# Third tile's input loaded in 32x32 squares and turned by VectorE, with its first norm's sums by ones-products

## The chip, the cores and the metric

One core of a Trainium2 chip runs the whole program. The metric is device microseconds (us) of one execution; the median of several executions stands for a kernel. TensorE (PE) does matrix products, VectorE (DVE) elementwise work, ScalarE (ACT) activations with a scale and a bias, GpSimd (POOL) almost nothing here, and SyncE (SP) issues nearly all transfers (DMA).

## The reference

The reference is one step of a two-layer encoder over two groups of frames, 1024 "prompt" rows and 32 "sample" rows, each 1024 channels wide, with shared weights. What matters for this change is its beginning:

```python
def rmsnorm(x, g):
    xf = x.astype(jnp.float32)
    y = xf * lax.rsqrt(jnp.mean(xf * xf, axis=-1, keepdims=True) + EPS)
    return (y * g.astype(jnp.float32)).astype(x.dtype)
...
    for i in range(DEPTH):
        mod = jax.nn.silu(c) @ w_ada[i] + b_ada[i]
        sh1, sc1, gt1, sh2, sc2, gt2 = jnp.split(mod[:, None, :], N_MOD, axis=-1)
        h = rmsnorm(x, g_norm[i, 0]) * (1 + sc1) + sh1
        ...
            mix, v = sgu_mixer(h, ...)      # z = gelu(h @ w_in); u, v = split(z); v is normed again
        ...
        x = x + gt1 * rmsnorm(mix, g_norm[i, 1])
        h = rmsnorm(x, g_norm[i, 2]) * (1 + sc2) + sh2
        f = jnp.square(jax.nn.relu(h @ ffn_w_up[i])) @ ffn_w_down[i]
        x = x + gt2 * rmsnorm(f, g_norm[i, 3])
```

All arrays are float32. The sum of squares of the first norm runs over the 1024 channels of each token.

## The kernel before

The 1056 tokens are cut into three tiles: tiles 0 and 1 hold 384 prompt tokens each (three blocks of 128), tile 2 holds 256 prompt tokens and the 32 sample tokens (288 in all). On chip a tile lies with channels on the partitions: `acc[t]` is `[128, 8, 16 + n]`, eight channel blocks of 128 by n tokens behind a halo of 16 columns. Each float32 operand of a product is split into a high and a low part (`hh`/`hl` for the activations, `wh`/`wl` for the weights), and a product takes three matmuls: hi*hi, hi*lo, lo*hi.

**Blocks and items.** The nine token blocks are numbered b = 0 to 8; block 8 is the 32 sample rows. `stream` is one list of transfers in the order of their issue on SP's queue: x blocks (`"x", b`), weights of the conditioning (`"ada"`, 512 KB each) and pieces of the mixer's input weights (`"v", p, q`: columns p*512 to p*512+511 of the v half, channel blocks 2q and 2q+1; 512 KB each). `issue()` issues items until the next one needs one of the three `raw` buffers and none is free; each "v" item takes one and gives it back when `do_w` has split it (ACT copies the high part, L440; DVE subtracts for the low part, L79). `stream_to` works the list down to a named item.

**How x comes in.** A block is loaded with tokens on the partitions (`x_rows`, one 4 KB row for each token; block 8 goes into `junk`, the tile that also takes the discarded squares). `do_x` lets ACT square each row and add it up along the row (`x_squares`, L585, sums in `ssx`); `x_turn` turns the block by TensorE against the identity (L600, eight 128x128 transposes for a block, into PSUM), and DVE and ACT copy the halves into `acc[t]` (L606, L608). `first_norm(t)` is a generator: `spread` makes the factor 1/rms for each token from the sums (three tokens' blocks in three columns; DVE and ACT on 128x3), lays it on diagonals (L739), and three products with ones (L743, `pb_h`) spread it over all partitions; `apply` then multiplies by the coefficients (DVE, `mt`), adds the shift (ACT, `hh`, L890) and takes the low part (DVE, `hl`).

**The order of the beginning** is written out by hand in a `tc.manual_schedule()` block: every instruction is issued in the order in which the code names it. While tiles 0 and 1 come in, `early_mm` does the products of piece p = 0 for blocks 0 to 4 (L988). Then come the remaining turns (`while x_turns: turn()`, blocks 6, 7 and 8), the first part of tile 2's norm, the products of piece 0 for block 5 (`v_mm`, L943 to L945, 24 matmuls), the spread of tile 2's factor, and the ends of the blocks (`v_end`: gelu L955, square with a sum L956, store to DRAM L957). Behind the block the framework's scheduler orders the instructions: `v_order` runs piece 1 over blocks 0 to 5, then pieces 0 and 1 over blocks 6 to 8, then pieces 2 and 3 over all blocks. PSUM has three buffers (`pd`) for these blocks, so a block's products wait until the block three before it has been read.

`Stat` is the kernel's other way to a norm, used in all later norms: ACT squares each channel block of `acc` (L761), DVE adds the eight squares (L79), ACT and DVE split the sum in two parts (L791, L79), and two products with ones over the partitions (L806) give each partition the sum over all 1024 channels. ACT then takes the reciprocal root and its square (L810, L811), and DVE does one Newton step.

At the very end of the program the kernel already has a load of the kind that the change introduces: `load_last` (L1400) reads nine transfers of 32 partitions by 32 by 32 values, with runs of 128 bytes, and `turn_x` turns them by `turn32`, VectorE's transpose of 32x32 squares.

Of the kernel before, what the change touches and what calls it, by code (L numbers as in the profile page):

```python
# [11 lines left out]
AF = mybir.ActivationFunctionType  # L12
# [3 lines left out]
P = 128  # L16
D = 1024
KB = D // P
SEQ = 1024
DEC = 32  # L20
# [3 lines left out]
HALO = 16  # L24
# [3 lines left out]
NT = len(TILES)  # L28
# [6 lines left out]
def tile_stream_encoder_step(  # L35
# [25 lines left out]
    nc = tc.nc  # L61
    act = nc.scalar.activation
# [23 lines left out]
    turn32 = on_dve(nc.vector.transpose, 0.1, 930.0)  # L86
# [10 lines left out]
    ncol = [p + s for _, p, s in TILES]  # L97
# [103 lines left out]
    def bring(func):  # L201

        act(out=junk1, in_=epsT, func=func)
# [27 lines left out]
    ssx = sums[:, 0:9]  # L231
# [9 lines left out]
    def add_w(key, ap, shape):  # L241
        stream.append(("w", key, ap, shape))
# [34 lines left out]
    def add_x(b):  # L277
        if b < 8:
            ap = x_prompt[0, b * P : (b + 1) * P, :]
        else:  # L280
            ap = x_sample[0]
        stream.append(("x", b, ap, None))

    def v_item(p, q):
        return (
            ("v", p, q),
            sgu_w_in[0][q * 256 : (q + 1) * 256, SGU + p * 512 : SGU + (p + 1) * 512].rearrange(
                "(k p) f -> p k f", p=P
            ),
            (2, 512),  # L290
        )

    def w_vpiece(p):
        for q in range(4):
            add_w(*v_item(p, q))
# [65 lines left out]
            for b in range(3, 6):  # L361
                add_x(b)
    first_ada = len(stream)
    for b in range(6, 9):
        add_x(b)
    w_vpiece(1)
    rest += [(add_ada, 0, j) for j in range(16, 40)] + [(add_wide, 0, j) for j in range(40, 48)]
    some_ada(8)
    for p in range(2, 4):
# [26 lines left out]
    def in_raw(k):  # L396
# [4 lines left out]

    x_rows = [
        room("h", t, f"x_rows{t}")
        .rearrange("p k n -> p (k n)")[:, : ncol[t] // P * D]
        .rearrange("p (b k n) -> p b k n", k=KB, n=P)
        for t in range(NT)
    ]
    junk = room("l", NT - 1, "xsq")

    def issue():  # L410
        while state["issued"] < len(stream):
            k = state["issued"]
            kind, key, ap, shape = stream[k]
            if in_raw(k):
                if state["raw"] == RAW_SLOTS:
                    return
                state["raw"] += 1
                r = t_raw(f"raw{k}")
            elif kind == "x":
                r = x_rows[key // 3][:, key % 3] if key < 8 else junk[:, :, P : 2 * P]  # L420
            else:
                r = work.tile([P, 1024], F32, tag="W", bufs=W_SLOTS, name=f"raw{k}")
            if kind == "x":
                nr = P if key < 8 else DEC
                i = nc.sync.dma_start(r[:nr], ap.rearrange("t (k n) -> t k n", n=P))
            else:
                i = nc.sync.dma_start(r.rearrange("p (a b) -> p a b", a=shape[0]), ap)
            raws[k] = r
            loads[key] = i.ins
            state["issued"] += 1  # L430
# [150 lines left out]
            n -= 1  # L581

    def x_squares(b, r):
        nr = P if b < 8 else DEC
        act(  # L585
            out=junk[:nr, :, :P],
            in_=r[:nr],
            func=AF.Square,
            accum_out=ssx[:nr, b : b + 1],
        )  # L590

    def x_turn(b, r):
        t = min(b // 3, 2)
        c0 = (b - 3 * t) * P
        nr = P if b < 8 else DEC
        for half in range(2):
            pt = (ps_up if b == 4 else ps_ms)(f"xT{b}_{half}")
            for i in range(4):
                k = half * 4 + i
                nc.tensor.transpose(  # L600
                    pt[:, i * nr : (i + 1) * nr], r[:nr, k, :], ident[:nr, :nr]
                )
            dst = acc[t][:, half * 4 : half * 4 + 4, HALO + c0 : HALO + c0 + nr]
            src = pt[:, : 4 * nr].rearrange("p (a b) -> p a b", a=4)
            if half == 0 or t == 0:
                nc.vector.tensor_copy(dst, src)  # L606
            else:
                act(out=dst, in_=src, func=AF.Copy)  # L608
# [2 lines left out]
    x_turns = deque()  # L611

    def do_x(b, r):
        x_squares(b, r)
        if b < 3:
            x_turn(b, r)
        else:
            x_turns.append(lambda: x_turn(b, r))
# [283 lines left out]
    def first_norm(t):  # L902
        n = ncol[t]
        nb = 3
        cp = t_c(f"r_h0_{t}")
        got = []
        yield from spread(t, ssx[:, 3 * t : 3 * t + nb], f"h0_{t}", got, cp)
        act(out=cp[:, :n], in_=got[0][:, :n], func=AF.Copy)
        yield "statistics"
        yield from apply(t, 0, 0, 0, cp, keep=True)  # L910

    def products(ps, n, terms):

        last = len(terms) - 1
        tick(3 * len(terms) * (0.004 + n / 2265.0))
        for i, (wh, wl, rh, rl) in enumerate(terms):
            mm(ps[:, :n], wh, rh, start=i == 0, stop=False)  # L917
            mm(ps[:, :n], wh, rl, start=False, stop=False)  # L918
            mm(ps[:, :n], wl, rh, start=False, stop=i == last)  # L919
# [27 lines left out]
    def v_end(ps, p, b):  # L947
        m = P if b < 8 else DEC
        vt = t_x(f"vt{p}_{b}", [P, 512])
        z = ps  # L950
        if b == 8:
            act(out=vt[:m, :], in_=ps[m : 2 * m, :], func=AF.Copy)
            tt(out=vt[:m, :], in0=vt[:m, :], in1=ps[:m, :], op=ALU.add)
            z = vt
        act(out=vt[:m, :], in_=z[:m, :], func=AF.Gelu_apprx_tanh)  # L955
        act(out=ps[:m, :], in_=vt[:m, :], func=AF.Square, accum_out=ssqv[:m, b, p : p + 1])  # L956
        nc.sync.dma_start(vd[b * P : b * P + m, p * 512 : (p + 1) * 512], vt[:m, :])  # L957

    def statistics(h):
        while next(h) != "statistics":  # L960
            pass

    def stream_to(kind, key):
        k = max(i for i, s in enumerate(stream) if s[0] == kind and s[1] == key)
        while state["next"] <= k:
            stream_step()
        run_deferred()
# [2 lines left out]


    early_ps = [ps_dn(f"pv0_{b}") for b in range(3)]
    h0, h1, h2 = (first_norm(t) for t in range(NT))

    def early_mm(bs, q):

# [19 lines left out]
    def early_end(bs):  # L996
        for b in bs:
            v_end(early_ps[b], 0, b)
# [9 lines left out]
    def turn():  # L1008
        x_turns.popleft()()
# [9 lines left out]
    with tc.manual_schedule():  # L1019
        load_vectors(nc.scalar, 2, slice(0, 2))  # L1020
        issue()
        load_vectors(nc.gpsimd, 0, slice(0, 1))
        load_vectors(nc.gpsimd, 1, slice(0, 1))
        load_vectors(nc.gpsimd, 2, slice(2, 4))
        bring(AF.Silu)
        stream_to("x", 0)
        turn_conditions()
        stream_to("x", 2)
        bring(AF.Sqrt)
        next(h0)  # L1030
        next(h0)
        stream_to("ada", (0, 4, 0))
        turn_vectors()
        stream_to("ada", (0, 4, 1))
        next(h0)
        statistics(h0)
        fold()
        next(h0)
        stream_to("ada", (0, 0, 1))
        fold()  # L1040
        stream_to("w", ("v", 0, 0))
        next(h0)
        late_hi.pop()()
        next(h0)
        lo()
        early_mm((0, 1, 2), 0)
        stream_to("x", 5)
        next(h1)
        turn()
        next(h1)  # L1050
        stream_to("ada", (0, 5, 1))
        turn()
        fold()
        next(h1)
        statistics(h1)
        turn()
        early_ps.extend(ps_up(f"pv0_{b}") for b in (3, 4))
        next(h1)
        row(h1)
        stream_to("ada", (0, 1, 1))  # L1060
        next(h0)
        early_mm((3,), 0)
        fold()
        early_mm((4,), 0)
        for q in range(1, 4):
            stream_to("w", ("v", 0, q))
            row(h0)
            lo()
            next(h1)
            row(h1)  # L1070
            if q == 3:
                stream_to("x", 8)
            early_mm((0, 1), q)
            if q < 3:
                conditions(q + 1)
                fold()
                next(h0)
            early_mm((2,), q)
            if q < 3:
                fold()  # L1080
            early_mm((3, 4), q)
        while x_turns:
            turn()
        next(h2)
        ps = ps_ms("pv0_5")
        v_mm(ps, 0, 5, range(KB))
        next(h2)
        next(h2)
        early_end((0,))
        stream_to("w", ("v", 1, 1))  # L1090
        early_end((1, 2))
        stream_to("w", ("v", 1, 2))
        early_end((3,))
        stream_to("w", ("v", 1, 3))
        early_end((4,))
        statistics(h2)
        v_end(ps, 0, 5)
        for _ in h2:
            pass

# [630 lines left out]
```

## Time and profile before

| | |
|---|---|
| median of 3 runs | 2165.44 us (2163.97 to 2165.93) |
| profiled execution, its own time | 2163.59 us |
| span of the profiled execution | 2161.8 us |
| granted TensorE clock | 0.999 |
| TensorE busy | 2143.9 us (99%) |
| VectorE busy | 1423.9 us (66%) |
| ScalarE busy | 981.9 us (45%) |
| DMA | 311.77 MB, mean 144 GB/s |

All times in the profile are us from the start of the span; the remaining 1.8 us of the execution lie outside it. A row of the timeline gives start, duration, engine, line, operation and tiles, and in brackets the idle time before it with what ended it. Consecutive matmuls overlap, so their rate is read from their starts and not from their durations.

### The profile page before, as it was taken

The page shows a single profiled execution, that of the slowest core. Times are in us where ns is not written, and L with a number is a line of the kernel's source. Part 1 is how long each engine was busy: PE and PEld are TensorE (multiplying, and loading weights), DVE is VectorE, ACT ScalarE, POOL GpSimd, SP SyncE. Part 2 cuts the span into 40 slices and gives each one's busy share as a digit, 9 for nine tenths or more (in the row PEclk, how much of TensorE's full clock was granted, in tenths as well). Part 3 has the DMA queues.
Part 4 walks back from the last instruction along what each step waited for, and adds up shares of the span by engine and source line. Part 5 has one row for each costly group of instructions (what it writes and reads, how often), then busy time and mean ns, then how long its engine had stood idle before and what let it go on. Part 6 is the DMA issues. An engine that isn't in the chain of part 4 may idle for free.

```text
span 2161.8 us, 33186 instructions
## 1 busy us (share of the span) xinstructions
PE 2143.9 (99%) x13214; PEld 2079.8 (96%) x13214; DVE 1423.9 (66%) x2520; ACT 981.9 (45%) x1667; POOL 7.9 (0%) x20
## 2 busy tenths in 40 slices
PE   8999999999999999999999999999999999999998
PEld 6878999999999999999999999999999999999998
DVE  6787738467778549576757779869685553523375
ACT  5634332233456652324345566656564542322454
POOL 0000000000000000000000000000000000000000
PEclk9999999999999999999999999999999999999999
DMA  8486524353447444344545466465454541302243
GB/s 299 153 269 209 168 82 136 96 153 107 133 126 220 127 147 146 98 117 137 175 127 164 143 192 200 148 193 164 141 161 133 166 149 58 108 20 69 78 137 120
DMA packets 363263, 311.77 MB, mean 144 GB/s; under 512 B 20099, under 2 KB 325803, under 8 KB 363109
## 3 DMA queue, kind: packets, MB, share of 16 engines
q1 hardware_dynamic: 362852, 309.43, 46.6%
q8 instruction: 103, 1.69, 0.3%
q14 instruction: 52, 0.42, 0.1%
q10 hardware_dynamic: 128, 0.14, 0.0%
q0 software_dynamic: 128, 0.09, 0.0%
HBM read 278.95 MB, written 30.66 MB: 143 GB/s over the span
## 4 chain that ended last, share of the span: by engine, by line
PE 96%; DVE 2%; DMA 1%; ACT 1%; issue 0%; POOL 0%; POOLq 0%; ACTq 0%; DVEq 0%
PE pf L917 11%; PE pg L917 11%; PE pf L919 11%; PE pf L918 11%; PE pg L919 11%; PE pg L918 11%; PE pu L917 3%; PE pu L919 3%; PE pu L918 3%; PE po L917 3%; PE po L918 3%; PE po L919 3%; PE pv L943 2%; PE pv L944 2%; PE pv L945 2%; PE psp L1263 1%
## 5 line engine op out<-in xcount | busy, mean ns | idle before, releaser
L917 PE MATMUL pg<-fh,wh_dn 128*128 128x384 f32 (+1 forms) x1536 | 496.1, 323 | 0.0
L917 PE MATMUL pf<-hh,wh_up 128*128 128x384 f32 (+1 forms) x1536 | 494.4, 322 | 0.0
L919 PE MATMUL pf<-hh,wl_up 128*128 128x384 f32 (+1 forms) x1536 | 493.0, 321 | 1.2 <-DVE wl_up L79 1.2
L918 PE MATMUL pf<-hl,wh_up 128*128 128x384 f32 (+1 forms) x1536 | 493.1, 321 | 0.0
L918 PE MATMUL pg<-fl,wh_dn 128*128 128x384 f32 (+1 forms) x1536 | 492.5, 321 | 0.0
L919 PE MATMUL pg<-fh,wl_dn 128*128 128x384 f32 (+1 forms) x1536 | 492.5, 321 | 0.0
L79 DVE TENSOR_TENSOR wl_up<-raw,wh_up 128x1024 fp32r<-128x1024 f32 x152 | 185.8, 1223 | 169.1 <-ACT wh_up L440 169.1
L919 PEld LDWEIGHTS pf<-hh,wl_up 128*128 128x128 f32 x1536 | 288.6, 188 | 1.9 <-DVE wl_up L79 1.9
L917 PEld LDWEIGHTS pg<-fh,wh_dn 128*128 128x128 f32 x1536 | 288.3, 188 | 1.5 <-ACT fh L1169 0.4
L440 ACT ACTIVATE wh_up<-raw 128x1024 fp32r<-128x1024 f32 x152 | 161.2, 1060 | 282.3 <-PE pf L918 217.7
L918 PEld LDWEIGHTS pg<-fl,wh_dn 128*128 128x128 f32 x1536 | 288.3, 188 | 0.9 <-DVE fl L79 0.2
L918 PEld LDWEIGHTS pf<-hl,wh_up 128*128 128x128 f32 x1536 | 288.3, 188 | 0.4
L917 PEld LDWEIGHTS pf<-hh,wh_up 128*128 128x128 f32 x1536 | 288.2, 188 | 0.4
L919 PEld LDWEIGHTS pg<-fh,wl_dn 128*128 128x128 f32 x1536 | 288.2, 188 | 0.0
L79 DVE TENSOR_TENSOR acc<-acc,pg 128x384 f32<-128x384 f32 (+1 forms) x336 | 173.7, 517 | 151.2 <-PE pg L919 150.5
L440 ACT ACTIVATE wh_dn<-raw 128x1024 fp32r<-128x1024 f32 x152 | 160.9, 1060 | 209.8 <-PE pg L918 171.4
L79 DVE TENSOR_TENSOR wl_dn<-raw,wh_dn 128x1024 fp32r<-128x1024 f32 x152 | 185.8, 1223 | 82.7 <-ACT wh_dn L440 82.6
L79 DVE SCALAR_TENSOR_TENSOR aa<-raw,csil,aa 128x512 f32<-128x512 f32 (+1 forms) x364 | 203.2, 619 | 7.6 <-DMA raw<-in_w_ada_dram 7.3
L1345 ACT ACTIVATE r<-pf 128x384 f32<-128x384 f32 (+1 forms) x192 | 86.5, 450 | 197.7 <-PE pf L919 197.7
L79 DVE TENSOR_TENSOR fl<-r,fh 128x384 fp32r<-128x384 f32 (+1 forms) x192 | 100.0, 521 | 85.7 <-ACT fh L1169 84.2
L917 PE MATMUL pu<-hh,wh_u 128*128 128x384 f32 (+1 forms) x384 | 125.9, 328 | 0.0
L917 PE MATMUL po<-ush,wh_o 128*128 128x384 f32 (+1 forms) x384 | 123.5, 322 | 0.0
(268 smaller groups left out, 2923.2 us busy)
## 6 DMA issues: line engine op xcount, KB each, us to landing
raw<-in_ffn_w_up_dram SPq DMA_DIRECT2D x152, 512.0 KB, 3.9
raw<-in_ffn_w_down_dram SPq DMA_DIRECT2D x152, 512.0 KB, 3.5
raw<-in_w_ada_dram SPq DMA_DIRECT2D x96, 512.0 KB, 4.4
raw<-in_sgu_w_in_dram SPq DMA_DIRECT2D x40, 512.0 KB, 4.2
xd<-acc SPq DMA_DIRECT2D x8, 1536.0 KB, 7.8
raw<-in_sgu_w_out_dram SPq DMA_DIRECT2D x24, 512.0 KB, 3.6
xo_r<-xd SPq DMA_DIRECT2D x32, 384.0 KB, 3.3
vd<-vt SPq DMA_DIRECT2D x32, 256.0 KB, 4.3
```

The lines of the kernel that those rows point to most:

```text
L79: return op(out, *args, **kw)
L440: act(out=wh, in_=r, func=AF.Copy)
L917: mm(ps[:, :n], wh, rh, start=i == 0, stop=False)
L918: mm(ps[:, :n], wh, rl, start=False, stop=False)
L919: mm(ps[:, :n], wl, rh, start=False, stop=i == last)
L943: mm(ps[:m, :], a_h, wh[:, o : o + 512], start=k == 0, stop=False)
L944: mm(ps[:m, :], a_h, wl[:, o : o + 512], start=False, stop=False)
L945: mm(ps[:m, :], a_l, wh[:, o : o + 512], start=False, stop=k == KB - 1)
L1263: mm(sp[:, c * P : (c + 1) * P], vl[:, c, k * P : (k + 1) * P], wr[:, c * P : (c + 1) * P], start=True, stop=True,)
L1345: act(out=r[:, :n], in_=ps[:, :n], func=AF.Relu)
```

## The change

Blocks 6, 7 and 8 are no longer loaded as rows. Each group of 32 tokens is loaded by four transfers, one for each a = 0 to 3, of 32 tokens (on partitions 32a to 32a+31) by 8 channel blocks by 32 channels, in runs of 128 bytes: 16 transfers for block 6, 16 for block 7, 4 for block 8. In the stream they stand between the four items of piece 1: block 6, v(1,0), block 7, v(1,1), block 8, v(1,2), v(1,3). Tile 2's data is turned by nine VectorE transposes of 128x8x32 (`turn32`) directly into `acc[2]`; TensorE's transposes, the row sums on ACT and the copies of blocks 6 to 8 are gone. The first norm of tile 2 goes by `Stat` in a new generator `last_first_norm`, with its reciprocal root taken on ACT. In the hand-written order, v(1,0) is split before the last `early_mm` calls, the gelu table is loaded by `bring` ahead of tile 2's squares, and block 5's `v_end` comes before the statistics of tile 2.

```diff
@@ stream
-    for b in range(6, 9):
-        add_x(b)
-    w_vpiece(1)
+    for q in range(4):
+        if q < 3:
+            add_x(6 + q)
+        add_w(*v_item(1, q))
@@ x_rows
-        .rearrange("p k n -> p (k n)")[:, : ncol[t] // P * D]
-        .rearrange("p (b k n) -> p b k n", k=KB, n=P)
+        .rearrange("p k n -> p (k n)")
+        .rearrange("p (b k n) -> p b k n", k=KB, n=P if t < NT - 1 else 32)
@@ issue
-                r = x_rows[key // 3][:, key % 3] if key < 8 else junk[:, :, P : 2 * P]
+                r = x_rows[min(key // 3, NT - 1)]
+                r = r[:, key % 3] if key < 6 else r
...
-            if kind == "x":
-                nr = P if key < 8 else DEC
-                i = nc.sync.dma_start(r[:nr], ap.rearrange("t (k n) -> t k n", n=P))
+            if kind == "x" and key < 6:
+                i = nc.sync.dma_start(r, ap.rearrange("t (k n) -> t k n", n=P))
+            elif kind == "x":
+                for j in range(ap.shape[0] // 32):
+                    for a in range(4):
+                        i = nc.sync.dma_start(
+                            r[32 * a : 32 * a + 32, 4 * (key - 6) + j],
+                            ap[32 * j : 32 * j + 32].rearrange("s (k a m) -> s a k m", a=4, m=32)[:, a],
+                        )
@@ x_squares, x_turn: the cases for the 32 rows of block 8 are dropped
...
     def do_x(b, r):
+        if b >= 6:
+            return
         x_squares(b, r)
@@ behind first_norm
+    def last_first_norm(t):
+        for j in range(ncol[t] // 32):
+            turn32(acc[t][:, :, HALO + 32 * j : HALO + 32 * j + 32], x_rows[t][:, j])
+        yield False
+        st = Stat(t, f"h0_{t}")
+        for k in range(KB):
+            st.square(k)
+        yield False
+        got = []
+        yield from st.finish(got)
+        yield "statistics"
+        yield from apply(t, 0, 0, 0, got[0], keep=True)
...
-    h0, h1, h2 = (first_norm(t) for t in range(NT))
+    h0, h1 = (first_norm(t) for t in range(2))
+    h2 = last_first_norm(2)
@@ the hand-written order
             if q == 3:
-                stream_to("x", 8)
+                stream_to("w", ("v", 1, 0))
             early_mm((0, 1), q)
...
-        while x_turns:
-            turn()
+        bring(AF.Gelu_apprx_tanh)
+        next(h2)
         next(h2)
         ps = ps_ms("pv0_5")
         v_mm(ps, 0, 5, range(KB))
-        next(h2)
-        next(h2)
         early_end((0,))
         stream_to("w", ("v", 1, 1))
         early_end((1, 2))
...
         early_end((4,))
+        v_end(ps, 0, 5)
         statistics(h2)
-        v_end(ps, 0, 5)
         for _ in h2:
             pass
```

More of the change, by code (lines that the diff above doesn't have):

```diff
@@ L583, in x_squares @@
     def x_squares(b, r):
[L584 to L590, printed above, removed]
+        act(out=junk[:, :, :P], in_=r, func=AF.Square, accum_out=ssx[:, b : b + 1])
     def x_turn(b, r):
-        t = min(b // 3, 2)
+        t = b // 3
         c0 = (b - 3 * t) * P
-        nr = P if b < 8 else DEC
         for half in range(2):
@@ L599, in x_turn @@
                 k = half * 4 + i
[L600 to L604, printed above, removed]
+                nc.tensor.transpose(pt[:, i * P : (i + 1) * P], r[:, k, :], ident)
+            dst = acc[t][:, half * 4 : half * 4 + 4, HALO + c0 : HALO + c0 + P]
+            src = pt.rearrange("p (a b) -> p a b", a=4)
             if half == 0 or t == 0:
```

## The prediction

> **What bounds the kernel now.** I read the page's busy times first, then its chain, and then the timelines of the four engines around the change, 30 to 80 us.
>
> ```profile
> PE 2143.9 (99%) x13214; PEld 2079.8 (96%) x13214; DVE 1423.9 (66%) x2520; ACT 981.9 (45%) x1667; POOL 7.9 (0%) x20
> PE 96%; DVE 2%; DMA 1%; ACT 1%; issue 0%; POOL 0%; POOLq 0%; ACTq 0%; DVEq 0%
> ```
>
> TensorE works for 2143.9 of 2161.8 us, and 96% of the chain that ended last is TensorE. So a change pays by the TensorE time that it takes away, and costs by the TensorE idle time that it makes. The order behind the hand-written part is the same but for a few neighbours swapped up to about 155 us, so I take an earlier TensorE to stay earlier until the end, us for us. The stretch is this one, in the timeline of TensorE (start, duration):
>
> ```profile
> 57.29 1.07 PE L988 MATMUL pv<-wl_v,hh 128*128 128x512 f32 x4
> 58.20 2.04 PE L600 MATMUL xT<-ident,x_rows 128*128 128x128 f32 x16
> 60.17 0.72 PE L600 MATMUL xT<-ident,xsq 32*128 32x32 f32 x8
> 60.99 0.50 PE L943 MATMUL pv<-wh_v,hh 128*128 128x512 f32 x1
> ...
> 66.38 0.40 PE L945 MATMUL pv<-wh_v,hl 128*128 128x512 f32 x1
> 66.61 0.94 PE L743 MATMUL pb_h<-r_h,ones 128*128 128x128 f32 x6
> 67.48 0.50 PE L943 MATMUL pv<-wh_v,hh 128*128 128x512 f32 x1
> 67.97 0.50 PE L944 MATMUL pv<-wl_v,hh 128*128 128x512 f32 x1
> ```
>
> From the end of `early_mm` (58.20) to the first matmul of piece 1 (67.48) TensorE spends 2.79 us on tile 2's transposes, 5.62 us on the 24 matmuls of block 5 (0.23 us each), and 0.87 us on the spread `pb_h`. After its first matmul, piece 1 stands still for 0.26 us more (67.48 to 67.97 instead of 0.23).
>
> **What goes.** The transposes and `pb_h`: 2.79 + 0.87 = 3.66 us of TensorE. What comes on TensorE is two products with ones over 288 columns, 0.30 us each:
>
> ```profile
> L806 PE MATMUL pn_rs<-sc_rs,ones 128*128 128x288 f32 x1 | 0.3, 300 | 0.0
> L761 ACT ACTIVATE sq_rs<-acc 128x288 f32<-128x288 f32 x8 | 3.4, 440 | 1.8 <-DVE acc L79 1.8
> L79 DVE TENSOR_TENSOR sq_rs<-sq_rs 128x288 f32<-128x288 f32 x7 | 3.2, 452 | 0.0
> L791 ACT ACTIVATE sc_rs<-sq_rs,eps 128x288 fp32r<-128x288 f32 x1 | 0.5, 538 | 0.5 <-DVE sq_rs L79 0.5
> L79 DVE SCALAR_TENSOR_TENSOR sm_rs<-sq_rs,eps,sc_rs 128x288 fp32r<-128x288 f32 x1 | 0.5, 515 | 0.0
> ```
>
> So the most that can be won is 3.66 - 0.60 + 0.26 + some 0.1 of overlap, about 3.4 us. That is under 0.2% of the time (4.3 us), which is about what a measurement of this kernel can tell from no change. What is left of it depends on three things: when the squares of x land, how long the new chain on VectorE and ScalarE is, and what ScalarE's new order holds up.
>
> **When x lands.** SP's queue in this stretch, then the landings of two of these transfers (KB, us from issue to landing), then two windows (busy time of each engine, clock, DMA share, GB/s):
>
> ```profile
> 30.74 2.17 SPq L427 DMA_DIRECT2D raw<-in_sgu_w_in_dram  x1
> 32.96 1.11 SPq L425 DMA_DIRECT2D x_rows<-in_x_prompt_dram  x2
> 34.11 0.71 SPq L425 DMA_DIRECT2D xsq<-in_x_sample_dram  x1
> 34.93 17.71 SPq L427 DMA_DIRECT2D raw<-in_sgu_w_in_dram  x3
> ...
> raw<-in_sgu_w_in_dram SPq DMA_DIRECT2D x1, 512.0 KB, 8.5
> x_rows<-in_x_prompt_dram SPq DMA_DIRECT2D x1, 512.0 KB, 7.8
> ...
> 30.00:40.00 10.00, 9.85 (x69) 6.68 (x69) 7.54 (x19) 4.33 (x9) 0.00 (x0) 1.00 1.07 398
> 40.00:50.00 10.00, 10.00 (x70) 7.41 (x69) 6.50 (x16) 4.67 (x9) 0.00 (x0) 1.00 0.41 123
> ```
>
> Until 40 us the transfers are full (the DMA share is 1.07, 398 GB/s), and SP issues about one a microsecond, each held until the transfer eight before it has landed. From 40 us the share is 0.41: there is room. In the changed kernel the first eight squares take the places of the old x rows, from 32.96 on, behind what is queued, and the ninth waits for the piece issued at 30.74, which lands at about 40 (30.74 + 8.5 from the start of its issue). From there SP issues 30 more transfers: 8 squares, v(1,0), 16 squares, v(1,1), 4 squares. Their pace is nowhere in this stretch. I bound it by two other places of the trace, four 64 KB loads issued back to back and two loads of 1024 runs of 128 bytes (the end of the kernel has nine of these; each is four of the new ones):
>
> ```profile
> 148.09 0.43 SPq L1193 DMA_DIRECT2D wt<-in_sgu_w_s_dram  x1
> ...
> 149.53 0.46 SPq L1196 DMA_DIRECT2D bs<-in_sgu_b_s_dram  x1
> 2066.34 1.32 SPq L1400 DMA_DIRECT2D xraw<-xtd  x2
> q1 hardware_dynamic: 1687, 0.21, 42.3%
> cache<-in_cache_pool_dram SPq DMA_DIRECT2D x2, 30.0 KB, 2.5
> ```
>
> Four issues from 148.09 to 149.53 make 0.48 us each, the two of 1024 runs 0.66 us each. I take 0.48, because a new one has a quarter of the runs. The fourth row is of the window 2066.3 to 2069.5, in which only those loads moved: 42.3% of 16 engines for 3.2 us over 1687 packets is 12.8 ns for 128 bytes, so one new transfer (256 packets) occupies the engines for 0.2 us, less than its issue. A 30 KB load lands in 2.5 us. The last square is then on chip at 40 + 30 x 0.48 + 2.5 = 56.9 us; at 0.66 it is 62.3.
>
> **The new chain.** It starts when VectorE and ScalarE are through with the last pieces of tile 1 and with v(1,0):
>
> ```profile
> 47.14 1.05 ACT L440 ACTIVATE wh_v<-raw 128x1024 fp32r<-128x1024 f32 x1
> 50.98 1.22 DVE L79 TENSOR_TENSOR wl_v<-raw,wh_v 128x1024 fp32r<-128x1024 f32 x1
> 52.76 1.15 ACT L890 ACTIVATE hh<-mt,mod 128x384 fp32r<-128x384 f32 x2 [2.37 <-DVE mt L79]
> 53.41 1.15 DVE L79 SCALAR_TENSOR_TENSOR hl<-mt,mod,hh 128x384 fp32r<-128x384 f32 x2 [0.16 <-ACT hh L890]
> 63.06 1.28 ACT L955 ACT_TABLE_LOAD   x1
> 64.36 0.60 ACT L955 ACTIVATE vt<-pv 128x512 f32<-128x512 f32 x1
> 65.62 1.99 ACT L440 ACTIVATE wh_v<-raw 128x1024 fp32r<-128x1024 f32 x2
> 89.66 0.76 DVE L79 STREAM_TRANSPOSE raw<-aa 128x256 f32<-128x256 f32 x2
> 90.35 0.60 DVE L79 SCALAR_TENSOR_TENSOR hl<-mt,mod,hh 128x256 fp32r<-128x256 f32 x2
> ```
>
> v(1,0) is issued after 16 squares, at about 44, so it is there at 53.9. ScalarE ends its `hh` at 53.9, the high part of v(1,0) at 54.9, and loads the gelu table (1.28) until 56.2; VectorE takes the low part (1.22) until 56.1. The nine turns are of 256 columns like the row at 89.66, two of which give way after 0.69 us: 9 x 0.35 = 3.2, until 59.3. The squares of x at 56.9 are in time for that; they are late from a pace of 0.55 us on. Then eight squares on ScalarE, 0.40 each back to back (between the row's 0.44 and 0.34 if it overlaps like the wider forms): 62.6. The last addition ends at 63.1, the split's first part (0.54) at 63.65, its second (0.52) at 64.2. TensorE, without the transposes, has block 5 done at 58.20 + 5.6 = 63.8, its first product with ones at 64.1, the second at 64.5.
>
> **What ScalarE holds up.** Piece 1 block 0 needs the PSUM buffer of piece 0 block 0, which ScalarE now reads only after the chain: gelu and square, 1.26 us (64.36 to 65.62 in the rows above), from 63.65 to 64.9. TensorE starts piece 1 at 64.9, 2.6 us earlier than before. Its eighth matmul there now is block 1's first, by the changed kernel's order of instructions. It waits for ScalarE's high part of v(1,1) (64.9 to 65.9) and the next gelu and square, until 67.2, while seven matmuls end at 66.5: 0.7 us idle. The low parts of v(1,2) and v(1,3) come out within 0.1 us of their use: 0.1 more. Before, that place lost 0.26. The gain is 2.6 - 0.8 + 0.26, so 2.0 us.
>
> **What is moved later.** Tile 2's factor now needs two more table loads on ScalarE (reciprocal root, then gelu again), behind the end of block 5.
>
> ```profile
> 75.28 0.60 ACT L955 ACTIVATE vt<-pv 128x512 f32<-128x512 f32 x1 [2.06 <-DMA vd<-vt]
> 76.97 0.65 DVE L79 SCALAR_TENSOR_TENSOR mt<-acc,coef,r_h 128x256 f32<-128x256 f32 x2 [1.35 <-ACT r_h L908]
> 91.38 0.72 ACT L890 ACTIVATE hh<-mt,mod 128x256 fp32r<-128x256 f32 x2 [1.05 <-DVE mt L79]
> ```
>
> Block 4's gelu waited until 75.28 for a store of SP's queue that stood behind v(1,3); v(1,3) is now ahead of all stores, so that I put this gelu at about 72. Two ends of blocks at 1.26, two loads at 1.28 and some 2.4 for root, gelu, square and VectorE's two steps put the factor at 79.5, where the first row with it was at 76.97. Tile 2's last `hh` (92.1 before) comes at about 95. TensorE needs tile 2 from 64.9 + 0.8 + 6 x 5.5 = 98.7 on, so 3 us of cover hide this. Of VectorE's additions (nine turns, seven sums, about 6 us, against 2.5 of copies and small steps dropped) all lie in a stretch where it was idle from 54.6 to 58.8 and from 62.1 to 66.7: no cost.
>
> **The sum.** The profiled execution took 2163.59 us, 1.85 under the median of 2165.44. Less 2.0 that is 2161.6 for an execution like it, and 2163.4 for a median.
>
> **Rivals.** *Late squares, slower.* If a new transfer costs SP not 0.48 us but what the full queue costs here, landing time over eight in flight, 7.8 / 8 = 0.98, then the last square lands at 40 + 30 x 0.98 + 2.5 = 71.9. The ninth turn starts 13 us later than 58.9, and ScalarE, VectorE and TensorE all stand in line behind it, since the gelu of block 0, the split of v(1,1) and the ones-products come after it on their queues. That is 2.0 - 13.0, a loss of 11 us: 2176.4. At 0.66 us it would be 1.4 us slower than before (2166.8); it decides from 0.55, and passes 0.2% at 0.76. For it: 36 transfers stand in place of three on one queue. Against it: the share of 0.41 from 40 us on, and 2.5 us for a small load, which with eight in flight is 0.31, below the issue. [...]
>
> *A longer chain, about no change.* If ScalarE's squares, the hand-overs between engines or the store that frees block 4's buffer take 2 us longer than the rows say, TensorE stands at the ones-products, and the gain is 0 plus or minus 1: 2165.4.
>
> *All of it.* If piece 1 finds ScalarE ready, 3.4 us: 2162.0. Against it speaks the gelu behind the split.
>
> **How the numbers follow.** Forecast (1 to 3 us won) 0.53, late squares 0.21, longer chain 0.15, all of it 0.11. Faster by over 0.2% would need all of it and the runs' scatter of 1 us: 0.07. Slower by over 0.2%: late squares from 0.76 us of pace on, 0.19. Within 0.2%: 0.74. The range reaches from all of it less 0.5 of scatter, 2161.5, past the pace of 0.66 (2166.8) and into the late squares up to 0.75, 2169.5; the forecast's own is 2162.3 to 2164.5.
>
> **What would show it.** Right: the last turn on VectorE at about 59.3, with no wait for a transfer of more than 1 us before it; the first matmul of piece 1 at 65, block 6 of piece 1 without a wait near 98.7. Wrong: a wait of the turns for `in_x_prompt_dram` beyond 60, issues of the squares over 0.55 us apart, or TensorE idle for more than 2 us between 63 and 75 or near 98.

## The result, and the profile after

| | before | changed |
|---|---|---|
| median of 22 runs each, us | 2163.32 (2162.48 to 2165.93) | 2166.88 (2165.86 to 2168.03) |
| ratio, 95% interval | | 1.0015 [1.0009, 1.0021] |
| profiled execution, us | 2163.59 | 2165.90 |
| its span, us | 2161.8 | 2164.1 |

The change makes the kernel 0.15% slower, 3.56 us by the medians. The forecast was 2.0 us faster. TensorE's busy time fell by 1.6 us, about half of the 3.1 that the change takes off (3.66 less 0.60), since the matmuls at half clock, shown below, last longer (3.56 us for nine, 0.40 each, against 7.60 for 35, 0.22 each); its share of the chain fell by a point, and SP's queue is new there (page of the changed kernel, busy times and chain):

```profile
PE 2142.3 (99%) x13186; PEld 2078.3 (96%) x13186; DVE 1429.2 (66%) x2531; ACT 982.6 (45%) x1667; POOL 7.9 (0%) x20
PE 95%; DVE 2%; DMA 2%; SPq 1%; ACT 1%; issue 0%; POOL 0%; POOLq 0%; DVEq 0%; ACTq 0%
```

The timeline of TensorE in the changed kernel (start, duration; in brackets the idle time before and what ended it), from the last of `early_mm` to the first matmul of piece 1, and on to the first of block 8:

```profile
57.79 1.07 PE L1004 MATMUL pv<-wl_v,hh 128*128 128x512 f32 x4
58.70 0.39 PE L958 MATMUL pv<-wh_v,hh 128*128 128x512 f32 x1
...
63.91 0.39 PE L960 MATMUL pv<-wh_v,hl 128*128 128x512 f32 x1
67.50 0.40 PE L808 MATMUL pn_h<-sc_h,ones 128*128 128x288 f32 x1 [3.20 <-ACT sc_h L793]
68.05 0.40 PE L808 MATMUL pn_h<-sm_h,ones 128*128 128x288 f32 x1 [0.16 <-DVE sm_h L79]
68.74 0.60 PE L958 MATMUL pv<-wh_v,hh 128*128 128x512 f32 x1 [0.28 <-ACT pv L971]
...
114.24 0.39 PE L950 MATMUL pv<-wh_v,hs 128*64 128x512 f32 x1
```

The transposes are gone: block 5 starts at 58.70, right behind `early_mm`. But the products with ones wait 3.20 us for ScalarE's part of the split. Piece 1 starts 10.04 us after `early_mm` (68.74 less 58.70); before it was 9.28 (67.48 less 58.20). That is 0.8 us of the loss; the larger part comes behind it:

```profile
64.20:67.50 3.30, 0.10 (x2) 1.00 0.17 66
68.70:72.30 3.60, 3.56 (x9) 0.54 0.27 82
72.40:80.00 7.60, 7.60 (x35) 1.00 0.83 243
```

These are windows of the changed kernel (length, TensorE's busy time and matmuls, granted clock, DMA share, GB/s). Behind its wait, which I call a stand, TensorE gets half its clock for 3.4 us (69.0 to 72.4), and does nine matmuls in 3.6 us, where 35 take 7.6 us later. Block 8 begins 55.5 us behind `early_mm`, against 53.5 before, by this row of the kernel before (111.66 less 58.20):

```profile
111.66 0.39 PE L935 MATMUL pv<-wh_v,hs 128*64 128x512 f32 x1
```

That distance is used below for every version, since the start-up ahead of it moves by up to 1.6 us from one profile to the next. Why the products wait stands in the timelines of SP, VectorE and ScalarE of the changed kernel, one after another:

```profile
32.98 12.34 SPq L431 DMA_DIRECT2D x_rows<-in_x_prompt_dram  x16
45.42 0.53 SPq L436 DMA_DIRECT2D raw<-in_sgu_w_in_dram  x1
46.00 10.33 SPq L431 DMA_DIRECT2D x_rows<-in_x_prompt_dram  x16
56.44 0.53 SPq L436 DMA_DIRECT2D raw<-in_sgu_w_in_dram  x1
57.02 3.08 SPq L431 DMA_DIRECT2D x_rows<-in_x_sample_dram  x4
```

```profile
56.53 2.40 DVE L79 STREAM_TRANSPOSE acc<-x_rows 128x256 f32<-128x256 f32 x7
59.56 0.45 DVE L79 STREAM_TRANSPOSE acc<-x_rows 128x256 f32<-128x256 f32 x1 [0.63 <-DMA x_rows<-in_x_prompt_dram]
61.76 0.45 DVE L79 STREAM_TRANSPOSE acc<-x_rows 128x256 f32<-128x256 f32 x1 [1.75 <-DMA x_rows<-in_x_sample_dram]
63.04 3.83 DVE L79 TENSOR_TENSOR sq_h<-sq_h 128x288 f32<-128x288 f32 x7 [0.84 <-ACT sq_h L763]
67.48 0.52 DVE L79 SCALAR_TENSOR_TENSOR sm_h<-sq_h,eps,sc_h 128x288 fp32r<-128x288 f32 x1 [0.60 <-ACT sc_h L793]
```

```profile
62.24 2.78 ACT L763 ACTIVATE sq_h<-acc 128x288 f32<-128x288 f32 x8 [5.36 <-DVE acc L79]
66.91 0.53 ACT L793 ACTIVATE sc_h<-sq_h,eps 128x288 fp32r<-128x288 f32 x1 [1.90 <-DVE sq_h L79]
67.35 0.58 ACT L970 ACTIVATE vt<-pv 128x512 f32<-128x512 f32 x1
```

SP issues the second sixteen squares in 10.33 us, 0.65 us each, without a wait between them, though each lands some 2.4 us after its issue, so that only about four are under way. It is through with the last square at 60.10. VectorE waits for it until 61.76. ScalarE waits 5.36 us ahead of its squares, with the ends of blocks 0 to 2 ready behind them in its queue. VectorE's seven additions take 3.83 us, one after another (each adds into the same tile), so ScalarE waits 1.90 us again before the split. Only then (67.35) comes the gelu that frees piece 1's first buffer.

### The profile page after: what moved, and what is told of

Its sections match the earlier page's. It is cut to its first block, busy times and chain, and to the rows that moved or that the text cites. A ratio compares the mean times of both kernels' runs of the same rounds, so it can differ in the third digit from the quotient of the medians.

```text
span 2164.1 us, 33199 instructions
## 1 busy us (share of the span) xinstructions
PE 2142.3 (99%) x13186; PEld 2078.3 (96%) x13186; DVE 1429.2 (66%) x2531; ACT 982.6 (45%) x1667; POOL 7.9 (0%) x20
## 4 chain that ended last, share of the span: by engine, by line
PE 95%; DVE 2%; DMA 2%; SPq 1%; ACT 1%; issue 0%; POOL 0%; POOLq 0%; DVEq 0%; ACTq 0%
PE pf L932 11%; PE pf L934 11%; PE pf L933 11%; PE pg L932 11%; PE pg L934 11%; PE pg L933 11%; PE po L932 3%; PE po L934 3%; PE po L933 3%; PE pu L932 3%; PE pu L934 3%; PE pu L933 3%; PE pv L958 2%; PE pv L960 2%; PE pv L959 2%; PE psp L1277 1%
```

## The experiments

Two theories stood against each other. *Late squares and a longer chain*: SP's 36 issues bring the last square too late, the sums take longer than I reckoned, and TensorE stands at the products with ones. *ScalarE*: what costs is the new order on ScalarE and its two more table loads. Each set of runs has its own runs of the kernel before. "Distance" is that from the end of `early_mm` to block 8's first matmul.

| version | median, us | kernel before | ratio, 95% interval | distance, us |
|---|---|---|---|---|
| before | | 2163.32 | | 53.5 |
| changed | 2166.88 | 2163.32 | 1.0015 [1.0009, 1.0021] | 55.5 |
| e1: 12 transfers | 2163.8 | 2163.14 | 1.0002 [0.9994, 1.0011] | 53.1 |
| e2: wait filled | 2166.81 | 2163.14 | 1.0017 [1.0008, 1.0025] | 56.1 |
| e3: no table loads | 2167.58 | 2163.14 | 1.0017 [1.0008, 1.0026] | 55.7 |
| e4: rows, new norm | 2164.85 | 2163.14 | 1.0006 [0.9997, 1.0015] | 54.0 |
| e5: other order | 2162.34 | 2163.48 | 0.9997 [0.9988, 1.0006] | 52.7 |
| e6: e5 with 12 transfers | 2161.63 | 2163.48 | 0.9989 [0.9980, 0.9998] | 49.9 |
| e8: e4 with that order | 2162.93 | 2163.48 | 0.9997 [0.9988, 1.0006] | 52.5 |
| e9: e6, start kept busy | 2160.39 | 2164.19 | 0.9983 [0.9974, 0.9992] | 49.8 |
| e10: before, start kept busy | 2163.48 | 2164.19 | 0.9998 [0.9989, 1.0007] | 53.5 |
| e11: changed, start kept busy | 2167.19 | 2164.19 | 1.0015 [1.0006, 1.0024] | 57.6 |

**e1, twelve transfers instead of 36.** Token 4s+j goes to square j, so that one transfer brings a partition group of four squares; the turns write with a step of four.

```diff
-                for j in range(ap.shape[0] // 32):
-                    for a in range(4):
-                        i = nc.sync.dma_start(
-                            r[32 * a : 32 * a + 32, 4 * (key - 6) + j],
-                            ap[32 * j : 32 * j + 32].rearrange("s (k a m) -> s a k m", a=4, m=32)[:, a],
+                nj = ap.shape[0] // 32
+                for a in range(4):
+                    i = nc.sync.dma_start(
+                        r[32 * a : 32 * a + 32, 4 * (key - 6) : 4 * (key - 6) + nj].rearrange("p j k m -> p (j k) m"),
+                        ap.rearrange("(s j) (k a m) -> s a (j k) m", j=nj, a=4, m=32)[:, a],
...
```

> The changed kernel with the same squares in 12 transfers instead of 36 (token 4s+j of a block goes to square j, so that the four squares of one a are one transfer of 1024 runs of 128 bytes); everything else as in the changed kernel. My theory (late last square, at 0.65 us of issue for each transfer, then a chain of sums that is longer than its rows, then half clock for 3.4 us): the last square lands before 52, the ninth turn ends at about 59.7 instead of 62.2, TensorE's wait at the ones-products falls from 3.2 to about 1 us and the granted clock stays at 1.00 or drops for less; 2.5 to 4 us faster than the changed kernel, about 2163 to 2164.5, so within 1 us of the kernel before. Rival (the order on ScalarE and the table loads cost the time, the squares' landing is covered): no more than 0.5 us faster than the changed kernel.

Measured 2163.8 us, 3.1 us under the changed kernel's median and 0.7 over the kernel before: as expected. SP is through with x at 48.2, the nine turns run from 55.91 in 4.06 us without a wait, and the sums start at 60.82 instead of 63.04. In the timelines of SP, VectorE and TensorE, one after another:

```profile
40.80 3.96 SPq L431 DMA_DIRECT2D x_rows<-in_x_prompt_dram  x4
...
45.71 2.52 SPq L431 DMA_DIRECT2D x_rows<-in_x_sample_dram  x4
```

```profile
55.91 4.06 DVE L79 STREAM_TRANSPOSE acc<-x_rows 128x256 f32<-128x256 f32 x9
60.82 3.84 DVE L79 TENSOR_TENSOR sq_h<-sq_h 128x288 f32<-128x288 f32 x7 [0.85 <-ACT sq_h L765]
```

```profile
65.28 0.40 PE L810 MATMUL pn_h<-sc_h,ones 128*128 128x288 f32 x1 [1.64 <-ACT sc_h L795]
```

TensorE still stands 1.64 us, though no square is late any more. That part is the chain's; about 1 us of it is e1's own, since its turns, which write with the step of four, come every 0.45 us (4.06 / 9), where the changed kernel's take 0.34 (2.40 / 7).

**e2, the wait filled.** Thirteen matmuls into an unused bank between block 5 and the products with ones, to keep TensorE's clock.

```diff
+        idle = ps_ms("idle")
+        wh, _ = witem[("v", 0, 3)]
+        for i in range(13):
+            mm(idle, hh[1][:, 7, :P], wh[:, 512:], start=i == 0, stop=i == 12)
         early_end((0,))
```

> The changed kernel with 13 added matmuls of 128x512 into an unused PSUM buffer between block 5 and the ones-products (2.96 us of TensorE work whose result nobody reads). My theory: they only fill the wait of 3.2 us, TensorE no longer stands still for that long, the granted clock stays at 1.00 behind it instead of 0.54 between 68.7 and 72.3, and the eight matmuls that took 0.43 instead of 0.23 us run at 0.23; 0.8 to 1.7 us faster than the changed kernel (2165.2 to 2166.1) though it does more work. Rival (the slow matmuls hid behind ScalarE's wait for piece 1's splits anyway): no change, or slower by up to 0.5 us.

Measured 2166.81: no gain; my number was wrong, and the time is the rival's. The clock is whole now, but TensorE waits in piece 1 instead. Windows of e2, as above, and its list of TensorE's waits from 60 to 80 us (us in all, times, longest):

```profile
68.00:70.00 2.00, 1.43 (x5) 1.00 0.30 116
70.00:72.00 2.00, 1.68 (x8) 1.00 0.04 15
72.00:74.00 2.00, 1.27 (x6) 1.00 0.52 132
```

```profile
PE pv L958 <- ACT wh_v L449: 0.7, 1, 0.7
PE pv L959 <- DVE wl_v L79: 0.6, 2, 0.3
```

ScalarE and VectorE, with ends of blocks and splits queued behind the sums, set the pace there. But e2 does not decide between the two: the framework's scheduler put piece 1's matmuls, from the eighth on, in another order than in the changed kernel. e1 and e4 have the changed kernel's order and the whole clock there, and take 44.59 us from the first matmul of piece 1 to block 8 (66.52 to 111.11 in e1, 68.91 to 113.50 in e4); the changed kernel takes 45.50 (68.74 to 114.24). So the half clock costs it about 0.9 us, and in e2's order the waits cost more than that (46.17 us, 69.36 to 115.53).

**e3, no table loads.** Tile 2's root is replaced by a square, and the two table loads of 1.28 us around the root (79.64 and 81.36 in ScalarE's timeline of the changed kernel) are gone from e3's; tile 2's factor is then another number, and the rest of the work is the same.

```diff
-            act(out=r, in_=pn[:, :n], func=AF.Abs_reciprocal_sqrt, scale=1.0 / D)
+            root = AF.Square if self.tag == "h0_2" else AF.Abs_reciprocal_sqrt
+            act(out=r, in_=pn[:, :n], func=root, scale=1.0 / D)
```

> The changed kernel without the two table loads around tile 2's first reciprocal root: the root is replaced by a square there (the factor of tile 2's first norm is another number, the work is otherwise the same), so ScalarE has 2.6 us less and tile 2's factor comes some 3 us earlier. My theory: all of that is covered, TensorE reaches block 6 of piece 1 only near 100 us; within 0.5 us of the changed kernel (2166.9). Rival (the late factor and the late ends of piece 1's first blocks hold TensorE up): 1.5 to 2.6 us faster.

Measured 2167.58: no gain, the table loads are covered. The ScalarE theory falls in this part.

**e4, the new norm alone.** x by rows and TensorE's transposes as in the kernel before; squares, additions and products with ones as in the changed one, in its order.

```diff
     def do_x(b, r):
-        x_squares(b, r)
+        if b < 6:
+            x_squares(b, r)
...
-    h0, h1, h2 = (first_norm(t) for t in range(NT))
+    h0, h1 = (first_norm(t) for t in range(2))
+    h2 = last_first_norm(2)        # the changed kernel's, without the turns
```

> Half of the change: x in rows and TensorE's transposes as before, but tile 2's first norm by squares over the channels and ones-products, in the changed order, with v(1,0) split early. My theory: TensorE keeps the 2.79 us of transposes and loses only pb_h; tile 2's data is complete near 61, the chain of squares and sums ends near 67 while block 5 ends at 66.7, TensorE waits for under 1 us and keeps its clock; piece 1 starts at 67.5 to 68.5, so 0 to 1 us slower than the kernel before (2163.3 to 2164.5). Rival (the new norm and the order on ScalarE are the loss): 2 us or more slower than before, like the changed kernel.

Measured 2164.85, 1.7 us over the kernel before (interval from -0.6 to +3.2): between the two theories. The distance grew by 0.5 us. TensorE does not wait for the sums here, since the transposes (2.8 us) and block 5 cover them; the new norm costs little, and where it costs, it is by ScalarE's late ends of blocks, as its list of waits from 60 to 80 us says:

```profile
PE pv L955 <- ACT pv L968: 0.6, 2, 0.3
```

The profiled execution of e4 also lost 1.3 us ahead of the change, in the start-up (its `early_mm` ends at 59.50, before at 58.20; see e9). How much of the 1.7 us that is in the median is not shown.

**e5, another order.** If the squares are late only for what stands in line behind them, that work can go first. ScalarE ends blocks 0 to 2 and splits v(1,1) ahead of the squares; the split of the sums (in `Stat.square`) becomes a step of its own; TensorE begins piece 1's blocks 0 and 1 ahead of the products with ones.

```diff
         next(h2)                           # eight turns
+        early_end((0, 1))
+        stream_to("w", ("v", 1, 1))
+        early_end((2,))
         next(h2)                           # the last turn
         ps = ps_ms("pv0_5")
         v_mm(ps, 0, 5, range(KB))
-        early_end((0,))
-        stream_to("w", ("v", 1, 1))
-        early_end((1, 2))
+        next(h2)                           # the squares, the additions
+        early_end((3,))
+        next(h2)                           # the split of the sums
+        first = [ps_dn(f"pv1_{b}") for b in range(2)]
+        for b in range(2):
+            v_mm(first[b], 1, b, range(4))
         stream_to("w", ("v", 1, 2))
-        early_end((3,))
+        early_end((4,))
         stream_to("w", ("v", 1, 3))
-        early_end((4,))
         v_end(ps, 0, 5)
         statistics(h2)
...
```

> The changed kernel with its 36 loads, another order around the sums: the ends of blocks 0, 1 and 2 and the split of v(1,1) stand on ScalarE ahead of tile 2's squares (where it waited 5.36 us for the last square of x), the split's VectorE half stands in front of the last turn (where VectorE waited 1.75 us), and TensorE does k 0 to 3 of piece 1's blocks 0 and 1 (24 matmuls, 5.5 us) between block 5 and the ones-products. My theory (the late squares cost only because TensorE's and ScalarE's next work stands behind them): no wait of TensorE over 0.6 us at the ones-products, its clock at 1.00 from 60 to 80, and block 8's first matmul 2.5 to 4 us earlier behind the early matmuls than in the changed kernel (51.5 to 53.0 us instead of 55.5); time 2162.5 to 2164.5 where the changed kernel gave 2166.9, so 0 to 1 us under the kernel before. Rival (the gain is given back in piece 1, as with the filled gap, since ScalarE and VectorE limit it): 2165.5 to 2167.

Measured 2162.34, 4.5 us under the changed kernel's median (2166.88, from another set of runs), and 1.1 us under the kernel before, which its interval does not tell from nothing. The time is 0.2 us under my range; the distance, 52.7, is in it. TensorE's timeline in e5, and ScalarE's:

```profile
69.34 0.40 PE L813 MATMUL pn_h<-sc_h,ones 128*128 128x288 f32 x1 [0.40 <-ACT sc_h L798]
71.54 0.51 PE L968 MATMUL pv<-wl_v,hh 128*128 128x512 f32 x1 [0.76 <-DVE wl_v L79]
```

```profile
61.05 1.06 ACT L449 ACTIVATE wh_v<-raw 128x1024 fp32r<-128x1024 f32 x1 [2.50 <-DMA raw<-in_sgu_w_in_dram]
63.76 2.78 ACT L763 ACTIVATE sq_h<-acc 128x288 f32<-128x288 f32 x8 [0.40 <-DVE acc L79]
```

The wait for the sums is 0.40 us. But v(1,1), which stands behind 32 squares on SP's queue, keeps ScalarE waiting 2.50 us, and the splits behind it come late: TensorE waits 1.3 us for two of them, 0.76 for the longer. The 36 issues still cost, now by the weight behind them.

**e6, this order with twelve transfers.** The loads of e1 and the order of e5.

> The order of e5 with the twelve loads of e1, so that the sums start 2.2 us earlier as well. If late squares are what e5 still pays for, this is 1 to 2 us under e5: 2161 to 2163, under both kernels. If with e5's order nobody waits for the squares any more, e5 and e6 agree within 0.6 us. Block 8's first matmul 50 to 52.5 us behind the early matmuls.

Measured 2161.63, 1.85 us under the kernel before, and the distance is 49.9: 3.6 us less than before. TensorE works without a wait (window of e6):

```profile
60.00:76.00 16.00, 15.95 (x71) 1.00 0.59 178
```

By the medians e6 is only 0.7 us under e5, by the distance 2.9. The profiled execution of e6 (2160.07) is one of three at 2159.1 to 2160.1, all with a mean granted clock of 0.999; the other eight runs lie at 2161.6 to 2162.5, seven of them with 0.998. e9 takes this up.

**e8, the order without the turn.** e4 with an order like e5's: does the order alone make the gain?

```diff
+        early_end((0, 1))
         while x_turns:
             turn()
...
+        for b in range(2):
+            v_mm(first[b], 1, b, range(4))
```

> e4 (x by rows, TensorE's transposes kept, the new norm) with an order like e5's: ends of blocks 0 and 1 ahead of the turns, k 0 to 3 of piece 1's blocks 0 and 1 ahead of the ones-products. It tells how much of e6's gain is the order's alone. My theory: TensorE did not wait in e4, so the order gives at most 1 us here: 2163.8 to 2165, and e6 stays 1.5 to 3 us under it, which is the 2.7 us of transposes that the turn on VectorE takes from TensorE. Rival (the order alone makes it): within 0.6 us of e6.

Measured 2162.93, distance 52.5. TensorE never waits here either, and still pays for the transposes:

```profile
58.55 2.04 PE L600 MATMUL xT<-ident,x_rows 128*128 128x128 f32 x16
60.52 0.72 PE L600 MATMUL xT<-ident,xsq 32*128 32x32 f32 x8
```

They last 2.8 us, and e6 is 2.6 us shorter in the distance. So by the distance the turn on VectorE is worth about what TensorE's transposes take, once nobody waits for it. The medians are 1.3 us apart, short of that and of the 1.5 to 3 us expected. And the order gives e8 more than the 1 us I allowed it: the distance falls by 1.5 us from e4's, and where e4 was 1.7 us over its kernel before, e8 is 0.55 under. So the gain has two parts, the order's and the transposes'.

**e9, e10, e11: the start kept busy.** The profiles of e2, e3 and e4 have TensorE's clock at half from about 18.2 to 21.7 us, far ahead of the change; those of the others don't. Their `early_mm` ends at 59.3 to 59.5 us, that of the others at 57.9 to 58.7. Windows of e4 and of e9:

```profile
18.00:22.00 4.00, 4.00 (x12) 0.57 1.09 384
```

```profile
18.00:22.00 4.00, 3.84 (x18) 1.00 1.10 387
```

e9 is e6, e10 the kernel before and e11 the changed kernel, each with six idle matmuls in TensorE's wait ahead of the first early matmul:

```diff
+        idle = ps_ms("idle")
+        for i in range(6):
+            mm(idle[:, :P], ones, ident, start=i == 0, stop=i == 5)
         early_mm((0, 1, 2), 0)
```

> e6 with six idle matmuls of ones by the unit matrix in TensorE's wait of 1.11 us ahead of the first early matmul (16.8 to 17.9). The profiles of e2, e3 and e4 show TensorE's clock at half from about 18.2 to 21.7 us, those of the others don't, and e6's runs fall into 2159.1 to 2160.1 and 2161.6 to 2162.5. My theory: that stretch follows on the start-up's waits, it comes in some executions and costs a kernel that is bound by TensorE 1.3 to 2 us; kept busy there, the clock stays at 1.00, and all runs gather in the lower group: median 2159.2 to 2160.6, 3 to 4 us under the kernel before. Rival (the groups have another cause, or the idle matmuls are too few): the median stays at 2161 to 2162.2, in two groups.

> The kernel before with the same six idle matmuls. By the theory of e9 its runs gather at the lower end of the kernel before, 2162.4 to 2163.2 median, 0.3 to 1 us under it, so that e9 stands 2.5 to 3.7 us under this one by the change, its larger transfers and its order alone. Rival: no difference from the kernel before within 0.3 us, with the same spread (2162.5 to 2165.5).

> The changed kernel with the same six idle matmuls. Its time from 46 us on is set by SP's issues and the squares behind them, which a slow start of TensorE does not reach. So by my theory the idle matmuls gain nothing here: 2166.2 to 2167.2. Rival (the start-up's half clock is a part of the changed kernel's loss): 2165 to 2166.

e9 measured 2160.39, 3.8 us under the kernel before, with nine of eleven runs from 2159.3 to 2161.4: the median as expected, the gathering only in part, as four runs lie in e6's lower group. e6 and e9 come from different sets of runs, and their intervals overlap, so that the gain by the kept start alone is not shown. No slower execution of e6 was profiled either: that the half clock parts its two groups is a reading of their mean clocks. e10 measured 2163.48, 0.7 us under its kernel before, with two runs of eleven at 2166.3 and 2166.9. The median is 0.3 over the numbers I gave, the difference larger than the rival's 0.3, and its interval holds no change: undecided. e11 gained nothing (2167.19): as expected. e9 is the quickest of all versions, and stands 3.1 us under e10, which has the same start.

e11 also suggests why the changed kernel's median is 3.56 us worse, where its profiled execution (2165.90, the second quickest of 22) is 2.3 us worse. e11's profiled execution is at its median. VectorE's last turn, TensorE's wait, and windows of TensorE:

```profile
62.39 0.45 DVE L79 STREAM_TRANSPOSE acc<-x_rows 128x256 f32<-128x256 f32 x1 [3.65 <-DMA x_rows<-in_x_sample_dram]
```

```profile
68.14 0.61 PE L808 MATMUL pn_h<-sc_h,ones 128*128 128x288 f32 x1 [4.57 <-ACT sc_h L793]
```

```profile
67.00:67.50 0.50, 0.00 (x0) 0.81 0.00 0
67.50:68.00 0.50, 0.00 (x0) 0.50 0.00 0
68.00:74.00 6.00, 5.79 (x13) 0.50 0.27 84
74.00:75.00 1.00, 1.00 (x6) 0.93 0.94 305
```

TensorE is there 0.7 us sooner, the last square comes 0.6 us later (62.39 against 61.76), TensorE stands 4.57 us, and the half clock lasts 6.8 us (from 67.3 to 74.1). From piece 1 to block 8, with the changed kernel's order of matmuls, it takes 46.15 us (69.38 to 115.53), 1.6 more than e1 and e4. The distance is 57.6. That the slower executions of the changed kernel went the same way is not shown, since none of them was profiled.

## Why the prediction was wrong, by its steps

**What bounds the kernel; what goes.** Right. Block 5 follows `early_mm` at once, TensorE's busy time fell, and the most that can be won (3.4 us) is about what e6 reaches in the distance (3.6) and e9 in the time (3.8, of which the kept start may be 0.7 by e10, whose interval holds no change). "Us for us until the end" held as well: from block 8 on, the kernel before takes 2050.1 us of its span (2161.8 less 111.66), the changed one 2049.9.

**When x lands.** This is the step that failed first. Until 40 us SP went as reckoned: the eighth square was issued at 39.55, just when the piece issued at 30.76, eight transfers before it, had landed (39.53). That each transfer is held so, as I wrote, is more than the traces show: up to 40 us, SP's list of waits has five for a landing in the changed kernel (0.3 to 0.9 us, three of them ahead of squares) and two in the kernel before (0.3 and 0.6 us). But for the pace from there on I had two rows, 0.48 us for each of four 64 KB loads and 0.66 for each of two with 1024 runs, and took 0.48 "because a new one has a quarter of the runs". Measured: 0.65 us (10.33 / 16), with 256 runs. So the issue goes by the bound that I set aside, and the last square was turned from 61.76 instead of being on chip at 56.9. The bound itself came out (at 0.66 I had 62.3), but in part by luck: it was of loads with 1024 runs, and four of those back to back take 0.99 us each in e1. That the full queue would hold each for 0.98 us, the late-squares rival at its dearest, is not so in this stretch. Fewer and larger transfers paid: e1, with 12 for the 36, gets back 3.1 us. For the 36, SP took 27.1 us, from 32.98 to 60.10.

**The new chain.** The second failure, and smaller. The turns, 0.35 us each (2.40 / 7), and the squares, 0.35 (2.78 / 8), are as reckoned or better. The additions are not: I had the last end 0.5 us behind the last square, as if ScalarE's squares set the pace. They take 0.55 us each, each behind the one before, 3.83 in all, and the last ends 1.9 us behind the last square (66.87 against 65.02). From the last turn's end to the split's first part I reckoned 4.35 us (59.3 to 63.65); it was 5.2 (62.2 to 67.44). With the squares early, in e1, it still left TensorE a stand, though of e1's 1.64 us about 1 is from its own slower turns.

The two failures add up: piece 1 starts 10.04 us behind `early_mm`, where the forecast had 6.7 (64.9 less 58.20). Of these 3.3 us, 2.4 come from the late squares (the last turn ends 3.5 us behind `early_mm`, not 1.1) and 0.9 from the chain.

**What ScalarE holds up.** The first half was right: from the split to piece 1 it takes 1.3 us (67.44 to 68.74; I had 1.26). The 0.7 us of idle at block 1 did not show, as the matmuls at half clock took longer than ScalarE. e2 brought such a wait to light. No term of the sum had the half clock, which costs about 0.9 us here. Nor did the step see that the late chain also delays five ends of blocks and three splits, and so fills ScalarE's queue for the next 10 us. From piece 1's start on the forecast was 0.5 us more than before (0.8 less 0.26); measured is 1.3 more (45.50 against 44.18, which is 67.48 to 111.66).

**What is moved later.** The sign was right, the cover held. The last `hh` of tile 2 ends at 99.5 instead of 95, and TensorE does not wait for it: from 55 to 110 us the list of its waits names only the three at the sums and at piece 1's start. e3 shows the table loads to be free.

**The rivals.** *Late squares* was the right one: its price at 0.66 us was 2166.8, and the median is 2166.88. That fits so well in part by luck, as it had neither the longer additions nor the half clock, and the kernel before, 2165.44 in the three runs that I reckoned from, lies 1.3 to 2.3 us lower in the later sets. Its point of decision, 0.55, held, and all three signs of being wrong that I had named came: a turn that waits beyond 60 (until 61.76, for the sample rows), issues 0.65 us apart, and TensorE idle for 3.20 us. *A longer chain* is true as a part. *All of it* is what the change gives when the transfers are larger and the order is mended (e6, e9).

## What to carry to other kernels

Taking work off the engine that bounds a kernel wins only if what replaces it arrives in time: compare the last transfer's issue, not only its bytes, with the moment at which the next engine is free. When a step moves to other engines, look at what stands behind it on their queues; here, work that was ready stood behind a wait of 5.4 us, and putting it first took back the loss (e5); with larger transfers as well it became the whole gain (e6). The chain of dependent additions cost its full sum here, seven times 0.55 us, while ScalarE handed over a square every 0.35.

## What the runs showed of the hardware

A stand of TensorE had a second price here: half its clock. The granted clock was 0.50 for 3.4 us behind a stand of 3.20 (changed kernel, 69.0 to 72.4), for about as long behind one of 3.35 (e3, from about 69.5), and for 6.8 us at one of 4.57 (e11, from 67.3, still within the stand, to 74.1); after 1.64 us (e1) it stayed at 1.00. In the start-up e2, e3 and e4 had it at half for about 3.4 us (18.3 to 21.7 in e3), where the same instructions had 1.00 in the kernel before, the changed one, e1, e5, e6 and e8. What sets off such a stretch, and why some executions meet it at the start-up and others don't, is not settled. Those three profiles differ earlier as well: sixteen transposes, at about 6.7 us, take 2.7 to 3.0 us in e2, e3 and e4 and 3.5 to 3.7 in the kernel before, the changed one, e1 and e6, against 2.04 later (58.20, before). A link between the two was not shown. In piece 1 the half clock cost about 0.9 us for the 3.4 of the changed kernel, and 1.6 for those 4.8 of e11's 6.8 that lie behind piece 1's start.

A transfer of 32 KB in 256 runs held SP's queue for 0.65 us, one of 128 KB in 1024 runs for 0.99 (e1, 3.96 / 4): the larger ones cost SP 0.25 us for 32 KB. Two of 1024 runs at the kernel's end took 0.66 each; why these are quicker was not tried.
